# Differential attention scores: the low-part products of two maps moved onto half of the rows each

## The chip, the core and the metric

The kernel runs on one core of a Trainium2 chip. The metric is the device time of one execution in microseconds (us). Five engines work side by side and meet through semaphores: TensorE (PE; its weight loads are shown as PEld), VectorE (DVE), ScalarE (ACT), GpSimd (POOL) and SyncE (SP, which here issues all DMA transfers).

## What is computed

One encoder layer over 1280 tokens (1024 of a prompt, 256 of a sample) of width 1024. The change touches the scores of the differential attention: eight heads, each with two maps `c`, and per map a product of queries and keys over a head width of 64.

```python
def diff_attention(q, k, v, lam):            # q, k: (B, T, 8 heads, 2 maps, 64)
    ...
        s = jnp.einsum('bqhcd,bkhcd->bhcqk', qblk, k).astype(jnp.float32)
        p = jax.nn.softmax(s, axis=-1)
        p = p[:, :, 0] - lam * p[:, :, 1]
        return jnp.einsum('bhqk,bkhe->bqhe', p.astype(v.dtype), v)
```

## The kernel before

Every float32 operand is held as two float32r parts, a high one and a low one with `x = high + low`, and a product is built in PSUM from matmuls of such parts. An earlier stage writes queries and keys to DRAM as `qd[n]` and `kd[n]`, with n = 0 for the high parts and n = 1 for the low ones.

The attention stage goes over 40 pairs: per head four blocks of 256 prompt queries against 1024 keys, and one block of 256 sample queries against 256 keys. Each pair is two units of 128 queries, so there are 64 wide units and 16 narrow ones. `Pair.scores` makes the scores of one unit (both maps), `probs` the softmax, the difference and the transposes, and `values` the product with the values of a pair four units later.

For the scores the head width of 64 fills only half of the 128 rows of the array, so high and low parts are stacked. `load_keys` makes one key tile per map, high keys on rows 0 to 63 and low keys on rows 64 to 127. `load_queries` makes two query tiles, each `[128, 2, 256]` with one plane per map: in `Q[0]` the high queries stand on both halves of the rows, in `Q[1]` the low queries do. One matmul with `Q[0]` (line 741) gives high x high + high x low, and one with `Q[1]` (line 742) gives low x high + low x low. A wide map has two key blocks of 512, so a wide unit has eight score matmuls of 128x512, all over 128 rows.

A map's scores stand in a PSUM tile of two banks; the pool `ps_s` has two such tiles, one per map. DVE takes the row maximum (line 743), then ACT the exponential (line 745), after which the tile is free.

Beside the attention run the fillers: matrix products that the attention doesn't need (lines 283, 286 and 287, in `gemm_fm`), which are dealt out between units by a budget of time per unit (`fill`). The first matmul of each is held behind `anchor[0]`, the last line-741 matmul that was written. The final order on each engine is set by the framework's scheduler, which takes what is ready in its own model of time, so the source order of a unit isn't the order on PE.

Of the kernel before, what the change touches and what calls it, by code (L numbers as in the profile page):

```python
# [9 lines left out]
F32 = mybir.dt.float32  # L10
F32R = mybir.dt.float32r
# [40 lines left out]
QB = 3  # L52
# [88 lines left out]
def encoder_layer_kernel(ctx: ExitStack, tc: tile.TileContext, i, y_out):  # L141
    nc = tc.nc
    V, S, G, PE, SP = nc.vector, nc.scalar, nc.gpsimd, nc.tensor, nc.sync
# [9 lines left out]
    def f32(ap):  # L153
        return ap.bitcast(F32)
# [4 lines left out]
    def dt_(name, shape):  # L159
        return dram.tile(shape, F32, tag=name, name=name)  # L160


    qd = dt_("qd", [2, NB, 128, T])
    kd = dt_("kd", [2, NB, 128, T])
# [27 lines left out]
    def pool(es, name, bufs, space=None, side=None):  # L192
        kw = {} if space is None else {"space": space}
        if side is not None:
            kw["side"] = side
        return es.enter_context(tc.tile_pool(name=name, bufs=bufs, reuse_waits="tile", **kw))
# [194 lines left out]
    def load_keys(h):  # L391
        K = []
        for c in range(2):
            hc = 2 * h + c
            k = kp.tile([128, T], F32R, tag="k", name="k")
            for n in range(2):
                SP.dma_start(f32(k[n * 64:n * 64 + 64]), kd[n, :, hc * 8:hc * 8 + 8, :])
            K.append(k)
        return (K,)

    def load_queries(h, q0):
        qs = []
        for m in range(2):
            z = kp.tile([128, 2, 256], F32R, tag=f"q{m}", name="q", bufs=QB)
            for half in (slice(0, 64), slice(64, 128)):
                for c in range(2):
                    hc = 2 * h + c
                    SP.dma_start(f32(z[half, c, :]), qd[m, :, hc * 8:hc * 8 + 8, q0:q0 + 256])
            qs.append(z)
        return qs  # L410

    def load_values(h):
# [10 lines left out]
    with ExitStack() as es:  # L423
# [188 lines left out]
        for n, (kind, b) in enumerate(steps):  # L612
            if n >= 3:
                if kind in FN:
                    plain(kind, b)
                elif kind == "v":
                    values_out(b)
                else:
                    heads_out(kind, b)
            if n == 4:  # L620
                for c, (h, l, w_) in enumerate(xop):
                    for m, z in enumerate((h, l)):
                        for k in range(0, 8, 4):
                            SP.dma_start(xd[m, k:k + 4, :, cs(c)].rearrange("k p t -> p k t"), f32(z[:, k:k + 4, :]))
            if n == 5:
                for k in range(0, 8, 2):
                    raw, h, l = (rot.tile([128, 2, M], d, tag=t, name="m" + t) for t, d in (("tab", F32), ("o", F32R), ("z", F32R)))
                    SP.dma_start(raw, i["memT"][:, k:k + 2, :])
                    split(h, l, raw, S, V)
                    for m, z in enumerate((h, l)):  # L630
                        SP.dma_start(memd[m, k:k + 2].rearrange("k p t -> p k t"), f32(z))
            if n in LRUAT:
                with tc.high_priority(offset=-LRUP):
                    recur(LRUAT.index(n))
            if n == HEADAT:
                lru.close()
                kp = pool(head_pools, "kq", KB, side="right")
                wv = pool(es, "wv", 3, side="right")
                heads[0] = load_keys(0)
                queries_of[0] = load_queries(0, 0)  # L640
# [18 lines left out]
    with ExitStack() as es:  # L659
# [11 lines left out]
        ps_s = pool(es, "psS", 2, PSUM)  # L671
# [38 lines left out]
        anchor = [None]  # L710
# [10 lines left out]
        class Pair:  # L721
            def __init__(self, h, q0, s0, nk):
                self.h, self.q0, self.s0, self.nk = h, q0, s0, nk
                self.nkt = nk // 128
                self.nth = (self.nkt + 3) // 4
                self.E = {}

            def scores(self, qt):
                K = self.ops[0]
                Q = self.Q  # L730
                nk = self.nk
                qs = slice(qt * 128, qt * 128 + 128)
                nm = sp.tile([128, 2], F32, tag="nm", name="nm")
                ss = sp.tile([128, 2], F32, tag="ss", name="ss")
                E = []
                for c in range(2):
                    ps = ps_s.tile([128, 1024], F32, tag="s", name="s")
                    for k0 in range(0, nk, 512):
                        n = min(512, nk)
                        ks = slice(self.s0 + k0, self.s0 + k0 + n)  # L740
                        anchor[0] = PE.matmul(ps[:, k0:k0 + n], Q[0][:, c, qs], K[c][:, ks], start=True, stop=False)
                        PE.matmul(ps[:, k0:k0 + n], Q[1][:, c, qs], K[c][:, ks], start=False, stop=True)  # L742
                    V.tensor_reduce(nm[:, c:c + 1], ps[:, :nk], axis=AX.X, op=ALU.max, negate=True)  # L743
                    e = ep.tile([128, 1024], F32, tag=f"e{c}", name="e")
                    S.activation(e[:, :nk], ps[:, :nk], AF.Exp, bias=nm[:, c:c + 1], accum_out=ss[:, c:c + 1])  # L745
                    E.append(e)
                self.E[qt] = (E, ss)

            def probs(self, qt):
                nk, nkt, nth = self.nk, self.nkt, self.nth  # L750
                E, ss = self.E.pop(qt)
                if qt == 0:
# [7 lines left out]
                V.scalar_tensor_tensor(self.s1q[:, qt:qt + 1], ss[:, 0:1], 1e-5, ss[:, 0:1], ALU.mult, ALU.mult)  # L760
                V.scalar_tensor_tensor(E[0][:, :nk], E[1][:, :nk], r, E[0][:, :nk], ALU.mult, ALU.add)
                for a in range(nth):
                    n = min(4, nkt)
                    ps = ps_t.tile([128, 4, 128], F32, tag="t", name="t")
                    for t in range(n):
                        kt = a * 4 + t
                        PE.transpose(ps[:, t, :], E[0][:, kt * 128:kt * 128 + 128], ident)
                    dh = self.pts[a][0][:, :, qt * 128:qt * 128 + 128]
# [40 lines left out]
        units = [(p, qt) for p in pairs for qt in range(2)]  # L809
        heads[0] += load_values(0)  # L810
        queries_of[1] = load_queries(0, 256)
        with tc.high_priority(offset=MEMP):
            mem = stored(memd, 0, M)
        done = 0.0
        for u in range(len(units) + VLAG):
            if u < len(units):
                p, qt = units[u]
                ahead = units[min(u + LEAD, len(units) - 1)][0].h
                if ahead not in heads:
                    with tc.high_priority(offset=-LOADP):  # L820
                        heads[ahead] = load_keys(ahead)
                later = units[min(u + LEADQ, len(units) - 1)][0]
                n_ = pairs.index(later)
                if n_ not in queries_of:
                    queries_of[n_] = load_queries(later.h, later.q0)
                p.ops = heads[p.h]
                p.Q = queries_of[pairs.index(p)]
                p.scores(qt)
                done += FILLT / 8.5 * (1 if p.nk == TP else 0.25)
            if 1 <= u <= len(units):  # L830
                p, qt = units[u - 1]
                p.probs(qt)
            if VLAG <= u and units[u - VLAG][1] == 1:
                p = units[u - VLAG][0]
                if len(heads[p.h]) == 1:
                    heads[p.h] += load_values(p.h)
                p.ops = heads[p.h]
                p.values()
            fill(done)
# [102 lines left out]
    with ExitStack() as es:  # L942
# [4 lines left out]
        for c0, n in CHUNKS:  # L947
# [5 lines left out]
            for b in range(8):  # L953
# [3 lines left out]
                ps = pp.tile([128, 512], F32, tag="mm", name="ps")[:, :n]  # L957
                for k in range(8):
                    wh, wl = (z[:, k * 128:k * 128 + 128] for z in ws[b])
                    h, l = (op[m][k // 2][:, k % 2, :] for m in range(2))  # L960
# [5 lines left out]
                m = st.tile([128, 2, 512], F32R, tag="m", name="m")[:, :, :n]  # L966
# [8 lines left out]
    with ExitStack() as es:  # L975
# [24 lines left out]
        with ExitStack() as es1:  # L1000
# [3 lines left out]
            kp = pool(es1, "kX", 2)  # L1004
# [4 lines left out]
            ps_s = pool(es1, "psS", 2, PSUM)  # L1009
# [106 lines left out]
    with ExitStack() as es:  # L1116
# [44 lines left out]
        with ExitStack() as es1:  # L1161
# [49 lines left out]
            for half_ in range(2):  # L1211
# [3 lines left out]
                for fs in groups:  # L1215
                    hs_ = []
                    for f in fs:
                        hs_.append(hidden(f, *((E_M1, E_SL1) if f == NF - 1 else (E_M, E_SL))))
                        if pending:
                            z, t = pending.pop()  # L1220
# [100 lines left out]
```

## Time and profile before

| | us |
|---|---|
| median of 3 runs | 2827.26 (2827.05 to 2828.02) |
| profiled execution, its own time | 2822.44 |
| span of that execution | 2820.5 |
| PE busy | 2739.3 (97%) |
| DVE busy | 1705.5 (60%) |
| ACT busy | 1138.6 (40%) |
| POOL busy | 919.3 (33%) |
| granted TensorE clock, mean | 0.993 |

The attention stage runs from 632.78 us (its first score matmul) to about 1333.6 us of the span. A time on PE is best read from the starts of neighbouring matmuls: the duration shown for one matmul reaches past the start of the next, since matmuls are pipelined and their ends are modelled.

### The profile page before, as it was taken

Reading aid. Unit: us, or ns where it says so; the run is one execution under the profiler, and the core shown is the slowest. Engines: PE = TensorE matmul, PEld = TensorE weight load, DVE = VectorE, ACT = ScalarE, POOL = GpSimd, SP = SyncE. Lnnn points to the kernel's source line nnn. Section 1 sums busy time; section 2 is a strip of 40 time slices with the busy share of each in tenths; the row PEclk is TensorE's granted clock in tenths of the full one; section 3 lists DMA queues with packets and bytes.
Section 4 is the critical chain, followed back from the end, with each engine's and each line's share of the span. In section 5 each row is a group of like instructions: output and inputs, shape, how many; then the busy total and the mean of one; then the engine's idle time right before and its main releaser. Section 6 shows DMA issues by size and latency. Waiting matters only on the chain.

```text
span 2820.5 us, 40319 instructions
## 1 busy us (share of the span) xinstructions
PE 2739.3 (97%) x15240; PEld 2411.8 (86%) x15240; DVE 1705.5 (60%) x2517; ACT 1138.6 (40%) x1921; POOL 919.3 (33%) x576
## 2 busy tenths in 40 slices
PE   9999999999999999999999999998999998999998
PEld 7888888887889888888788889887999997899997
DVE  4545667415667755644345576563677777577776
ACT  3656444415666655455211144321223333233232
POOL 0000000013345543344100100052566559565555
PEclk9999999999999999999999999999999999999999
DMA  9633545565567756844887576658322225622221
GB/s 358 208 109 112 175 152 190 174 206 178 162 202 222 244 169 199 252 141 162 303 273 235 172 276 210 217 186 299 116 79 90 83 82 193 227 84 80 79 80 60
DMA packets 292450, 496.26 MB, mean 176 GB/s; under 512 B 22560, under 2 KB 165664, under 8 KB 292256
## 3 DMA queue, kind: packets, MB, share of 16 engines
q1 hardware_dynamic: 292256, 493.69, 53.6%
q8 instruction: 120, 1.97, 0.3%
q14 instruction: 74, 0.61, 0.1%
HBM read 342.08 MB, written 151.52 MB: 175 GB/s over the span
## 4 chain that ended last, share of the span: by engine, by line
PE 67%; DVE 11%; DMA 11%; issue 4%; ACT 4%; POOL 2%; SPq 1%; DVEq 0%; ACTq 0%; POOLq 0%
PE ps L283 4%; PE ps L286 4%; PE ps L287 4%; PE ps L357 3%; PE ps L355 3%; PE ps L356 3%; PE ps L520 3%; PE ps L521 3%; PE ps L522 3%; PE o L1202 3%; PE o L1203 3%; PE o L1204 2%; PE ps L885 2%; PE ps L883 2%; PE ps L884 2%
## 5 line engine op out<-in xcount | busy, mean ns | idle before, releaser
L190 POOL TENSOR_TENSOR wl<-raw,wh 128x1024 fp32r<-128x1024 f32 x132 | 321.3, 2435 | 973.5 <-ACT wh L187 863.6
L187 ACT ACTIVATE wh<-raw 128x1024 fp32r<-128x1024 f32 (+1 forms) x224 | 224.4, 1006 | 492.0 <-PE ps L286 155.2
L520 PE MATMUL ps<-xh,wh 128*128 128x512 f32 (+1 forms) x768 | 274.4, 357 | 12.1 <-ACT xh L187 5.9
L355 PE MATMUL ps<-xbh,sh 128*128 128x320 f32 x880 | 273.1, 310 | 8.9 <-DMA sh<-fpd 7.0
L521 PE MATMUL ps<-xl,wh 128*128 128x512 f32 (+1 forms) x768 | 273.9, 357 | 0.5 <-DVE xl L190 0.5
L357 PE MATMUL ps<-xbh,sl 128*128 128x320 f32 x880 | 272.6, 310 | 0.4 <-DMA sl<-fpd 0.3
L522 PE MATMUL ps<-xh,wl 128*128 128x512 f32 (+1 forms) x768 | 273.0, 356 | 0.0
L356 PE MATMUL ps<-xbl,sh 128*128 128x320 f32 x880 | 272.4, 310 | 0.0
L283 PE MATMUL ps<-fh,wh 128*128 128x512 f32 (+1 forms) x704 | 258.6, 367 | 11.7 <-DVE g L705 5.0
L286 PE MATMUL ps<-fl,wh 128*128 128x512 f32 (+1 forms) x704 | 255.7, 363 | 2.5 <-DMA fl<-memd 2.5
L287 PE MATMUL ps<-fh,wl 128*128 128x512 f32 (+1 forms) x704 | 255.1, 362 | 0.0
L190 DVE TENSOR_TENSOR wl<-raw,wh 128x1024 fp32r<-128x1024 f32 (+1 forms) x136 | 177.5, 1311 | 96.6 <-ACT wh L187 84.7
L743 DVE TENSOR_REDUCE nm<-s 128x1 f32<-128x1024 f32 (+1 forms) x160 | 167.3, 1059 | 93.8 <-PE s L742 93.4
L1205 DVE SCALAR_TENSOR_TENSOR y<-y,o 128x512 f32<-128x512 f32 x200 | 133.5, 681 | 115.4 <-PE o L1204 108.0
L850 POOL TENSOR_TENSOR rstd<-rstd,mhalf 128x1 f32<-128x1 f32 x30 | 34.5, 1152 | 498.4 <-DVE rstd L849 498.4
L1202 PE MATMUL o<-wh,hh 128*128 128x512 f32 x440 | 175.0, 398 | 11.8 <-DVE wh L189 4.3
L745 ACT ACTIVATE e<-s,nm 128x1024 f32<-128x1024 f32 (+1 forms) x160 | 158.6, 996 | 57.6 <-DVE nm L743 55.7
L355 PEld LDWEIGHTS ps<-xbh,sh 128*128 128x128 f32 x880 | 165.8, 188 | 12.8 <-DMA sh<-fpd 8.4
L520 PEld LDWEIGHTS ps<-xh,wh 128*128 128x128 f32 x768 | 146.3, 190 | 34.3 <-ACT xh L187 5.9
L1203 PE MATMUL o<-wl,hh 128*128 128x512 f32 x440 | 173.1, 394 | 0.0
L356 PEld LDWEIGHTS ps<-xbl,sh 128*128 128x128 f32 x880 | 165.9, 189 | 3.8
L357 PEld LDWEIGHTS ps<-xbh,sl 128*128 128x128 f32 x880 | 165.7, 188 | 3.4 <-DMA sl<-fpd 0.9
(261 smaller groups left out, 7241.6 us busy)
## 6 DMA issues: line engine op xcount, KB each, us to landing
raw<-w_in SPq DMA_DIRECT2D x80, 512.0 KB
raw<-ffn_in SPq DMA_DIRECT2D x80, 512.0 KB
raw<-ffn_out SPq DMA_DIRECT2D x44, 512.0 KB
q<-qd SPq DMA_DIRECT2D x320, 64.0 KB
raw<-p_lru SPq DMA_DIRECT2D x24, 512.0 KB
qd<-hl SPq DMA_DIRECT2D x16, 640.0 KB
kd<-hl SPq DMA_DIRECT2D x16, 640.0 KB
vd<-v SPq DMA_DIRECT2D x40, 256.0 KB
```

The costliest lines, as they stand in the source:

```text
L190: leng.tensor_tensor(l, src, f32(h), ALU.subtract)
L283: ins = PE.matmul(ps, a, h, start=(k == 0), stop=False)
L286: PE.matmul(ps, a, l, start=False, stop=False)
L287: PE.matmul(ps, b, h, start=False, stop=(k == 7))
L355: PE.matmul(ps, w[n][0][:, ks], xb[m][0][:, k, :], start=(k == 0), stop=False)
L356: PE.matmul(ps, w[n][0][:, ks], xb[m][1][:, k, :], start=False, stop=False)
L357: PE.matmul(ps, w[n][1][:, ks], xb[m][0][:, k, :], start=False, stop=(k == 3))
L520: PE.matmul(ps, wh[:, ks], h[:, k, :], start=(k == 0), stop=False)
L521: PE.matmul(ps, wh[:, ks], l[:, k, :], start=False, stop=False)
L522: PE.matmul(ps, wl[:, ks], h[:, k, :], start=False, stop=(k == 7))
L1202: PE.matmul(ps, hs_[a][0][:, ts], wo[a][0][:, hs], start=(a == 0), stop=False)
L1203: PE.matmul(ps, hs_[a][0][:, ts], wo[a][1][:, hs], start=False, stop=False)
```

## The change

The low products are made on 64 rows instead of 128. The low queries of both maps stand in one tile: those of map 0 on rows 0 to 63, those of map 1 on rows 64 to 127. The keys of map 1 are stacked the other way, low keys on top and high keys below, so that each map's high keys lie on the same rows as its low queries. A low product then multiplies low queries with high keys alone; the term low x low is no longer computed. The number of score matmuls stays the same: four of 128 rows and four of 64 rows in a wide unit, two and two in a narrow one. Both PSUM tiles of a unit are taken ahead of its matmuls, the source writes all four high products first, then the low ones alternating between the maps, and after them the two row maxima and exponentials. A pair's queries come in six transfers instead of eight.

```diff
             k = kp.tile([128, T], F32R, tag="k", name="k")
             for n in range(2):
-                SP.dma_start(f32(k[n * 64:n * 64 + 64]), kd[n, :, hc * 8:hc * 8 + 8, :])
+                half = n if c == 0 else 1 - n
+                SP.dma_start(f32(k[half * 64:half * 64 + 64]), kd[n, :, hc * 8:hc * 8 + 8, :])
...
-        for m in range(2):
-            z = kp.tile([128, 2, 256], F32R, tag=f"q{m}", name="q", bufs=QB)
-            for half in (slice(0, 64), slice(64, 128)):
-                for c in range(2):
-                    hc = 2 * h + c
-                    SP.dma_start(f32(z[half, c, :]), qd[m, :, hc * 8:hc * 8 + 8, q0:q0 + 256])
-            qs.append(z)
+        zh = kp.tile([128, 2, 256], F32R, tag="qh", name="q", bufs=QB)
+        zl = kp.tile([128, 256], F32R, tag="ql", name="q", bufs=QB)
+        for n, half in enumerate((slice(0, 64), slice(64, 128))):
+            for c in range(2):
+                hc = 2 * h + c
+                SP.dma_start(f32(zh[half, c, :]), qd[0, :, hc * 8:hc * 8 + 8, q0:q0 + 256])
+            hc = 2 * h + n
+            SP.dma_start(f32(zl[half]), qd[1, :, hc * 8:hc * 8 + 8, q0:q0 + 256])
+        qs = [zh, zl]
...
+                pss = [ps_s.tile([128, 1024], F32, tag="s", name="s") for c in range(2)]
                 for c in range(2):
-                    ps = ps_s.tile([128, 1024], F32, tag="s", name="s")
-                    for k0 in range(0, nk, 512):
-                        n = min(512, nk)
-                        ks = slice(self.s0 + k0, self.s0 + k0 + n)
-                        anchor[0] = PE.matmul(ps[:, k0:k0 + n], Q[0][:, c, qs], K[c][:, ks], start=True, stop=False)
-                        PE.matmul(ps[:, k0:k0 + n], Q[1][:, c, qs], K[c][:, ks], start=False, stop=True)
+                    for k0, ks in keys:
+                        anchor[0] = PE.matmul(pss[c][:, k0:k0 + n], Q[0][:, c, qs], K[c][:, ks], start=True, stop=False)
+
+                for k0, ks in keys:
+                    for c, half in enumerate((slice(0, 64), slice(64, 128))):
+                        PE.matmul(pss[c][:, k0:k0 + n], Q[1][half, qs], K[c][half, ks], start=False, stop=True)
+                for c, ps in enumerate(pss):
                     V.tensor_reduce(nm[:, c:c + 1], ps[:, :nk], axis=AX.X, op=ALU.max, negate=True)
```

In the changed kernel the high products are line 743 and the low products line 747; the transposes of line 767 are line 773, and the value products of lines 785 to 787 are lines 791 to 793.

The order on PE at the second unit of the program, before. In the names `s_` is a map's PSUM tile, `k_4249` and `k_4252` are the keys of map 0 and map 1, and of the two `q_` tiles the first holds high queries and the second low ones:

```order
L286 MATMUL ps_5047<-fl_4969,wh_5042 128x512
L741 MATMUL s_5086<-k_4249,q_4255 128x512
L742 MATMUL s_5086<-k_4249,q_4260 128x512
L741 MATMUL s_5086<-k_4249,q_4255 128x512
L742 MATMUL s_5086<-k_4249,q_4260 128x512
L287 MATMUL ps_5047<-fh_4965,wl_5043 128x512
L741 MATMUL s_5094<-k_4252,q_4255 128x512
L742 MATMUL s_5094<-k_4252,q_4260 128x512
```

The same unit on PE in the changed kernel:

```order
L286 MATMUL ps_5041<-fl_4965,wh_5036 128x512
L743 MATMUL s_5078<-k_4249,q_4255 128x512 x2
L747 MATMUL s_5078<-k_4249,q_4256 128x512 x2
L287 MATMUL ps_5041<-fh_4961,wl_5037 128x512
L743 MATMUL s_5079<-k_4252,q_4255 128x512 x2
L747 MATMUL s_5079<-k_4252,q_4256 128x512 x2
L773 MATMUL t_5104<-ident_80,e_4995 128x128 x4
```

Here the two low products of one map follow each other, and those of the other map come later, behind a filler and that map's high products; the alternation of the source isn't kept.

A later unit on PE, before:

```order
L741 MATMUL s_7246<-k_6189,q_6586 128x512
L742 MATMUL s_7246<-k_6189,q_6591 128x512
L741 MATMUL s_7246<-k_6189,q_6586 128x512
L742 MATMUL s_7246<-k_6189,q_6591 128x512
L741 MATMUL s_7254<-k_6192,q_6586 128x512
L742 MATMUL s_7254<-k_6192,q_6591 128x512
```

The same unit on PE in the changed kernel, with map 0's tile `s_7220` and map 1's `s_7221`:

```order
L743 MATMUL s_7220<-k_6171,q_6566 128x512 x2
L743 MATMUL s_7221<-k_6174,q_6566 128x512 x2
L747 MATMUL s_7220<-k_6171,q_6567 128x512
L747 MATMUL s_7221<-k_6174,q_6567 128x512
L747 MATMUL s_7220<-k_6171,q_6567 128x512
L747 MATMUL s_7221<-k_6174,q_6567 128x512
L773 MATMUL t_7097<-ident_80,e_6895 128x128 x4
```

Here the order of the source is kept: the four low products stand together and alternate between the halves of the rows.

Over the whole stage the 256 wide low products stand on PE in 115 unbroken runs: 81 of two of the same map, 16 of four that alternate, 6 of three that alternate and 12 of one. The 32 narrow low products stand in 27: 22 of one and 5 of two, one of each map. A run is followed and preceded by matmuls over 128 rows; there are 142 in all.

## Rows read from the trace of the kernel before

**Rows 1.** The page: engine totals, then PE and its granted clock in 40 slices.

```profile
PE 2739.3 (97%) x15240; PEld 2411.8 (86%) x15240; DVE 1705.5 (60%) x2517; ACT 1138.6 (40%) x1921; POOL 919.3 (33%) x576
...
PE   9999999999999999999999999998999998999998
...
PEclk9999999999999999999999999999999999999999
```

**Rows 2.** Busy time by stretch: attention stage, then the stretch behind it.

```profile
core 0: us, PE busy (x) PEld busy (x) DVE busy (x) ACT busy (x) POOL busy (x), PEclk, DMA share, GB/s
632.78:1333.60 700.82, 687.95 (x4071) 600.72 (x4070) 417.00 (x680) 414.91 (x789) 304.98 (x179) 1.00 0.62 192
1333.60:1420.00 86.40, 79.49 (x367) 64.62 (x366) 34.50 (x46) 21.36 (x31) 15.16 (x11) 0.98 0.89 312
```

**Rows 3.** What PE waited for, 620 to 1335 us.

```profile
engine line waited for: us in total, times, longest us
PE pm L799 <- POOL rs L797: 2.9, 1, 2.9
PE ps L286 <- DMA fl<-memd: 2.5, 3, 0.9
PE ps L283 <- ACT mst L680: 1.5, 1, 1.5
PE ps L283 <- DMA fh<-xd: 1.3, 1, 1.3
PE ps L283 <- DMA fh<-lrud: 1.1, 3, 0.5
PE o L787 <- DMA vl<-vd: 1.0, 2, 0.8
```

**Rows 4.** Groups of PE instructions by line and shape, 632 to 1336 us.

```profile
L741 PE MATMUL s<-k,q 128*128 128x512 f32 x256 | 106.2, 415 | 1.0 <-DVE v L190 0.5 <-ACT e L745 0.4
L742 PE MATMUL s<-k,q 128*128 128x512 f32 x256 | 100.9, 394 | 0.0
...
L742 PE MATMUL s<-k,q 128*128 128x256 f32 x32 | 8.7, 283 | 0.0
```

**Rows 5.** PE in order of time: start us, duration us, then the instruction.

```profile
800.30 0.40 PE L742 MATMUL s<-k,q 128*128 128x512 f32 x1
800.54 0.28 PE L786 MATMUL o<-ptl,vh 128*128 128x256 f32 x1
...
801.38 0.28 PE L787 MATMUL o<-pth,vl 128*128 128x256 f32 x1
801.50 0.60 PE L686 MATMUL ps<-ident,mst 128*128 128x128 f32 x4
...
805.63 0.39 PE L283 MATMUL ps<-fh,wh 128*128 128x512 f32 x1
...
806.09 0.39 PE L287 MATMUL ps<-fh,wl 128*128 128x512 f32 x1
...
811.07 0.38 PE L799 MATMUL pm<-ident,rs 128*128 128x128 f32 x2
```

**Rows 6.** PE's weight loads in order of time, same columns.

```profile
805.86 0.19 PEld L287 LDWEIGHTS ps<-fh,wl 128*128 128x128 f32 x1
806.09 0.19 PEld L283 LDWEIGHTS ps<-fh,wh 128*128 128x128 f32 x1
```

**Rows 7.** PE in order of time behind a wait.

```profile
814.01 0.50 PE L741 MATMUL s<-k,q 128*128 128x512 f32 x1 [0.40 <-ACT e L745]
814.34 0.40 PE L742 MATMUL s<-k,q 128*128 128x512 f32 x1
```

**Rows 8.** The row maxima and the exponentials, each line's instructions: min/median/max ns.

```profile
L743 DVE TENSOR_REDUCE nm<-s x160: 410/1215/1226, 634.2 to 1331.5; 128x1 f32<-128x1024 f32 x128, 128x1 f32<-128x256 f32 x32
...
L745 ACT ACTIVATE e<-s,nm x160: 474/1117/1187, 647.6 to 1333.0; 128x1024 f32<-128x1024 f32 x128, 128x256 f32<-128x256 f32 x32
```

**Rows 9.** SP's issues of the query loads: min/median/max ns.

```profile
L408 SPq DMA_DIRECT2D q<-qd x320: 574/575/3442, 550.0 to 1276.8; - x160
```

More of the change, by code (lines that the diff above doesn't have):

```diff
@@ L401, in load_queries @@
     def load_queries(h, q0):
-        qs = []
-        for m in range(2):
-            z = kp.tile([128, 2, 256], F32R, tag=f"q{m}", name="q", bufs=QB)
-            for half in (slice(0, 64), slice(64, 128)):
-                for c in range(2):
-                    hc = 2 * h + c
-                    SP.dma_start(f32(z[half, c, :]), qd[m, :, hc * 8:hc * 8 + 8, q0:q0 + 256])
-            qs.append(z)
+        zh = kp.tile([128, 2, 256], F32R, tag="qh", name="q", bufs=QB)
[7 more added lines that the diff above has]
+        qs = [zh, zl]
         return qs
@@ L735, in scores @@
                 E = []
+                n = min(512, nk)
+                keys = [(k0, slice(self.s0 + k0, self.s0 + k0 + n)) for k0 in range(0, nk, 512)]
+                pss = [ps_s.tile([128, 1024], F32, tag="s", name="s") for c in range(2)]
                 for c in range(2):
-                    ps = ps_s.tile([128, 1024], F32, tag="s", name="s")
-                    for k0 in range(0, nk, 512):
-                        n = min(512, nk)
-                        ks = slice(self.s0 + k0, self.s0 + k0 + n)
-                        anchor[0] = PE.matmul(ps[:, k0:k0 + n], Q[0][:, c, qs], K[c][:, ks], start=True, stop=False)
-                        PE.matmul(ps[:, k0:k0 + n], Q[1][:, c, qs], K[c][:, ks], start=False, stop=True)
+                    for k0, ks in keys:
[4 more added lines that the diff above has]
+                for c, ps in enumerate(pss):
                     V.tensor_reduce(nm[:, c:c + 1], ps[:, :nk], axis=AX.X, op=ALU.max, negate=True)
```

## The prediction

> **What bounds the kernel now.** I read the engine totals first, then the stage, then PE's waits, then single matmuls. PE is busy in every slice of the span and its clock is at the higher level, 2.4 GHz, throughout [rows 1]. In the attention stage PE is busy for 687.95 of 700.82 us, while no other compute engine reaches 420 us [rows 2]. So the stage is a queue of PE work with 12.9 us of gaps in it. The table of waits says what the gaps are: singles of one to three microseconds, on a transfer, on POOL or on ACT, and none on the scores [rows 3]. A nanosecond that PE saves or loses in this stage therefore moves the end by about as much, and whatever happens on the other engines has to be large to count.
>
> What one matmul costs is read from starts, not from durations. Between 805.63 and 811.07 stand 24 matmuls of 512 columns, so one takes 5.44 / 24 = 0.227 us [rows 5]. Eight of 256 columns stand between 800.54 and 801.50, so one takes 0.12 us [rows 5]. The duration shown is 0.394 us [rows 4], so each matmul reaches 0.394 - 0.227 = 0.167 us into its successor; I call this its tail. The weight load of 0.19 us starts with the matmul ahead of its own and lies under it: the load for line 283 starts at 806.09, together with the line-287 matmul ahead of it [rows 5, 6]. Where no matmul covers it, it shows: behind a wait, a matmul of 512 columns at 814.01 is followed by the next at 814.34, which is 0.33 us instead of 0.227, so an uncovered load costs 0.10 us [rows 7].
>
> **The change part by part.** The number of score matmuls, their columns and their loads stay the same: 256 wide and 32 narrow low products before and after [rows 4]. Halving the rows of a matmul does not shorten it, as far as columns set the time: the 512 and the 256 columns above differ as their columns do. A gain can come only where two low products on different halves of the rows run at the same time.
>
> *How many can.* The source alternates the maps, but the order on PE decides, and there most low products of one map stand by themselves. From the runs counted in the section on the change, 16 of four give two such pairs each and 6 of three give one each: 38 wide pairs out of 128 possible. The 5 narrow pairs gain nothing that counts, because two loads take as long as two narrow matmuls: 0.12 us each is already what a matmul with its load takes. If a pair runs in the time of one matmul, the gain is 38 x 0.227 = 8.6 us. If it does not, the gain is 0.
>
> *What a switch costs.* There are 142 runs of low products, each entered from and left to matmuls over all 128 rows. That makes 284 places at which the array goes from one form to the other; the kernel before has none, its score rows all read 128*128 [rows 4]. This is the unknown price. The bound from below is 0: when the kind of operand changes, from a value product at 801.38 to a transpose at 801.50, the distance is the ordinary 0.12 us, so PE can change kind without a pause [rows 5]. The bound from above is a complete stop: the new form enters only when the tail of the old one is out, 0.167 us, and only then does its load begin, another 0.10 us, together 0.267 us. In between lie the two single prices: a load that can't be laid under a matmul of the other form, 0.10 us, or a tail that must run out while the load lies under it, 0.167 us. A change of form is unlike a change of operand kind: sums that ran through 128 rows have to leave after 64, while the matmul ahead is still in the same rows. That is why I do not take 0. The nearest rows are the two single prices, and I take their middle, 0.13 us: 284 x 0.13 = 36.9 us. The ends are 0 and 284 x 0.267 = 75.8 us.
>
> The Trainium skill, page "TensorEngine Tiling (Array Packing)", section Key Properties, says that changing the tiling mode, not just the tile, drains TensorE; it speaks against this change, gives no duration, and no run so far shows such a drain. The same page's table of speedups allows up to two times for a contraction of 64 rows; by it all 128 pairs would give 128 x 0.227 = 29.1 us, and this order on PE has only 38 of them.
>
> *PSUM tiles and the row maxima.* In the 16 alternating wide units map 0's row maximum starts some four matmuls later, about 0.9 us, than it did. Who waits: DVE's maximum (1.215 us), then ACT's exponential (1.117 us), then the next unit's first high product into that tile [rows 8]. PE has values, transposes and fillers to do in between, and no wait on the scores is among its longer ones [rows 3]. DVE and ACT are idle for 280 us each in the stage [rows 2]. Cost 0; if the cover failed in all 16 units it would be 16 x 0.9 = 14 us, which I hold unlikely.
>
> *Query loads.* Six transfers per pair instead of eight, 80 fewer; at 0.575 us each this takes 46 us off SP's queue [rows 9]. The weights of the fillers and the values stand in that queue, so they start earlier. PE's waits on transfers are fl 2.5, fh 1.3 and 1.1 and vl 1.0, together 5.9 us [rows 3]; that is the most it can give. These are first loads of a stage and not late queries, so I take 0. The keys stacked the other way are as many transfers of the same size.
>
> *Order.* The scheduler moves fillers by some places. The 12.9 us of gaps may come out a few microseconds smaller or larger, and a later stage end can lay up to some 5 of the 6.9 us that PE is idle in the stretch behind it under other work [rows 2]. I take 0, and about 4 us either way.
>
> **The sum.** 36.9 - 8.6 = +28.3 us, all in the attention stage. The profiled execution would go from 2822.4 to 2850.7 us. Its own time lies 4.8 us below the median of the runs, so the median goes from 2827.3 to about 2855 us. The single prices give the forecast's own range: 284 x 0.10 - 8.6 = +19.8 and 284 x 0.167 - 8.6 = +38.8, that is 2847 to 2866 us.
>
> **The rivals.**
>
> *A switch costs nothing and pairs run together (faster).* The mechanism is in the 38 pairs: 8.6 us less, 2818.7 us. For it speaks that PE changes between transposes, value products and scores without a pause [rows 5]. Against it speaks that none of those changes the rows in use. It decides below 8.6 / 284 = 0.030 us per switch; above that the change loses.
>
> *A switch is a complete stop.* 284 x 0.267 - 8.6 = +67.2 us, 2894 us. For it: after a wait PE does show the load uncovered [rows 7], and if a load of the other form may not enter rows in use, it comes behind the tail. Against it: loads are otherwise started a whole matmul ahead [rows 6].
>
> *The change does not do what it says.* PE goes on issuing one matmul after the other, without a stop and without running two at once: 0, 2827 us. For it: each low product has its own load, and two loads take 0.24 us, as long as one wide matmul, so the pair could be held up by its loads. Without pairs but with a switch price the time would be 2864 us, inside the forecast's own range.
>
> **How the numbers follow.** The forecast, a switch price somewhere around the two single prices, has a chance of 0.45; the complete stop 0.20; no price with pairs 0.20; nothing at all 0.15. About 0.2% of the time, 5.7 us, is what a measurement of this kernel can tell from no change. Slower: the forecast and the complete stop and a sliver of the rest, 0.66. Faster: most of the free pairs, 0.17. Same: nothing at all, and prices near the break-even, 0.17. The predicted time is the forecast's, 2855 us. To leave out no more than 2 in 10 the range has to reach from the free pairs to the complete stop, 2817 to 2895 us.
>
> **What would show it.** In the profile after, the step from a high product (line 743) to a low one (line 747), and from a low one to the next matmul over 128 rows, should be some 0.33 to 0.39 us instead of 0.227. Two low products of the same map should stand 0.227 us apart. In an alternating run the second product should start almost with the first, and the third about 0.23 us after it. The attention stage should end near 1362 us instead of 1333.6, with DVE, ACT and POOL busy as long as before. Steps of 0.227 everywhere would refute the switch price; 0.49 would be the complete stop. Wrong in another way would be low products that take longer than 0.227 us each, or new waits of PE on ACT at line 743: then the PSUM tiles, not the rows, would be what costs.

## The result and the profile after

The changed kernel takes 2857.66 us (median of 4 runs, 2856.66 to 2859.75), the kernel before beside it 2827.58 us: a ratio of 1.0111 (95% interval 1.0099 to 1.0123), 30 us more. The prediction was 2855 us, slower.

The engine totals of the changed kernel; against [rows 1] PE is 46 us busier, and no other engine by more than about 1 us:

```profile
PE 2785.0 (97%) x15240; PEld 2395.8 (84%) x15240; DVE 1703.2 (60%) x2517; ACT 1139.7 (40%) x1921; POOL 914.7 (32%) x576
```

The attention stage, from the first score matmul on, and the stretch behind it, with the columns of [rows 2]:

```profile
core 0: us, PE busy (x) PEld busy (x) DVE busy (x) ACT busy (x) POOL busy (x), PEclk, DMA share, GB/s
629.95:1374.00 744.05, 734.90 (x4079) 583.40 (x4078) 417.54 (x681) 417.05 (x789) 303.29 (x180) 1.00 0.57 177
1374.00:1460.00 86.00, 84.09 (x398) 69.65 (x399) 34.11 (x49) 21.82 (x33) 13.94 (x9) 1.00 0.87 309
```

About as many PE instructions as before (4079 against 4071) now need 744 us instead of 701, at the same clock, and DVE, ACT and POOL are busy as long as before [rows 2]. The time is lost on PE, in this stage.

Where it is lost stands in the order of time. First a run of two low products of the same map, PE and then its weight loads (start us, duration us; "x2" is two instructions in one row):

```profile
656.85 0.39 PE L287 MATMUL ps<-fh,wl 128*128 128x512 f32 x1
657.07 0.61 PE L743 MATMUL s<-k,q 128*128 128x512 f32 x2
657.62 0.73 PE L747 MATMUL s<-k,q 64*128 64x512 f32 x2
658.27 0.50 PE L283 MATMUL ps<-fh,wh 128*128 128x512 f32 x1
658.61 0.40 PE L286 MATMUL ps<-fl,wh 128*128 128x512 f32 x1
```

```profile
656.85 0.41 PEld L743 LDWEIGHTS s<-k,q 128*128 128x128 f32 x2
657.62 0.29 PEld L747 LDWEIGHTS s<-k,q 64*128 64x128 f32 x2 [0.35 <-issue]
658.27 0.19 PEld L283 LDWEIGHTS ps<-fh,wh 128*128 128x128 f32 x1 [0.36 <-issue]
658.38 0.19 PEld L286 LDWEIGHTS ps<-fl,wh 128*128 128x128 f32 x1
```

Two high products take 657.62 - 657.07 = 0.55 us instead of 2 x 0.227, and the two low ones 658.27 - 657.62 = 0.65 instead of 0.45; the filler behind them takes 0.34 instead of 0.227. The load rows say why. In [rows 6] a load starts a whole matmul ahead of its own. Here the load of the first low product starts only at 657.62, together with its matmul, after PEld stood still for 0.35 us; the load of the first matmul over 128 rows does the same at 658.27. So at a change of form no load starts under the matmul ahead: PE goes some 0.09 us past the ordinary step, and then loads without cover. In this trace the load starts together with its own matmul at all 284 switches. From the starts of single matmuls (the rows merge them), this run reads 0.319, 0.335, 0.322 and 0.337 us, where 0.227 each would be ordinary: 0.092 + 0.108 us for going in and 0.095 + 0.110 us for coming out, 0.20 us per switch. Over all 142 runs the median price of a run, with the gain of its pairs added back, is 0.41 us.

A run of four that alternate between the halves, PE and then its weight loads:

```profile
806.61 0.73 PE L747 MATMUL s<-k,q 64*128 64x512 f32 x4
807.28 0.66 PE L773 MATMUL t<-ident,e 128*128 128x128 f32 x4
```

```profile
806.61 0.30 PEld L747 LDWEIGHTS s<-k,q 64*128 64x128 f32 x4 [0.36 <-issue]
```

Four products take 0.67 us, as long as the two above: the second of each pair starts 3 or 4 ns after the first, and their four loads are through in 0.30 us, like the two above in 0.29. Pairs do run at the same time.

**Bookkeeping for all kernels below.** On PE I add up the distances from start to start in the attention stage, up to the first matmul of the merge stage behind it, and take off an ordinary distance for each matmul (0.227, 0.118, 0.109 and 0.11 us for 512, 256, 128 and 1 columns). What is left at the steps into, within and out of runs of low products over 64 rows, the step behind the first matmul after a run among them, I call their net cost, gains from pairs included; what is left anywhere else I call gaps. Before: gaps 35.3 us. After: net cost 48.0 us, gaps 21.4 us. These gaps are not the 12.9 us of the prediction: those are PE's idle time up to 1333.6 us, while the stage here reaches to 1393.9 us and every step over the ordinary one counts. PE's idle time alone is 19.8 us before and 11.1 us after in this longer stage.

### The profile page after: what moved, and what is told of

It is laid out like the page before. It is cut to its first block, busy times and chain, and to the rows that moved or that the text cites. A ratio compares the mean times of both kernels' runs of the same rounds, so it can differ in the third digit from the quotient of the medians.

```text
span 2858.0 us, 40191 instructions
## 1 busy us (share of the span) xinstructions
PE 2785.0 (97%) x15240; PEld 2395.8 (84%) x15240; DVE 1703.2 (60%) x2517; ACT 1139.7 (40%) x1921; POOL 914.7 (32%) x576
## 4 chain that ended last, share of the span: by engine, by line
PE 73%; DVE 10%; DMA 7%; issue 4%; ACT 3%; POOL 3%; SPq 0%; DVEq 0%; POOLq 0%; ACTq 0%
PE ps L283 5%; PE ps L286 5%; PE ps L287 5%; PE ps L523 3%; PE ps L522 3%; PE ps L524 3%; PE ps L355 3%; PE ps L357 3%; PE ps L356 3%; PE s L747 3%; PE o L1208 3%; PE o L1209 2%; PE o L1210 2%; PE ps L889 2%; PE ps L890 2%
```

## The experiments

Unless said otherwise, times are medians beside the kernel before on the same chip, with 95% intervals of the ratio.

### The order alone, over all rows (e1_all_rows)

```diff
 # changed kernel, with load_keys and load_queries of before
                 for k0, ks in keys:
-                    for c, half in enumerate((slice(0, 64), slice(64, 128))):
-                        PE.matmul(pss[c][:, k0:k0 + n], Q[1][half, qs], K[c][half, ks], start=False, stop=True)
+                    for c in range(2):
+                        PE.matmul(pss[c][:, k0:k0 + n], Q[1][:, c, qs], K[c][:, ks], start=False, stop=True)
```

> The changed kernel's way of writing a unit (both PSUM tiles taken first, four high products, then the low ones alternating, then the maxima), but with the loads of before and every low product over all 128 rows: no switch of form, no pairs. Theory 1, the price is in the rows (0.20 us per switch, 284 switches, pairs together): 2827.6 us, no change. Theory 2, part of the time is in the order (PE's gaps in the stage fell by 14 us in the trace of the changed kernel): about 2814 us. Theory 3, the loss comes from taking both PSUM tiles at once and the later row maxima, not from the rows: about 2858 us.

Measured: 2833.27 us against 2830.32, 1.0011 (1.0001 to 1.0022). Theory 3 falls: taking both PSUM tiles first and the maxima later costs 3 us, not 30. Theory 2 falls too: the gaps in the stage are 42.0 us, not shorter than before but longer. Part of that is the clock. In four stretches of this stage, 17.1 us together, the granted clock is 0.50, the lower level of 1.2 GHz, and wide matmuls stand 0.427 us apart instead of 0.227; before there is one such stretch, of 3.4 us. Half of PE's busy time in these stretches is an estimate of what that costs: 6.6 us of the gaps here and 1.7 us before. The loss is in the rows.

### Three ways of placing the low products (e2_pairs, e3_per_map, e4_each)

In each of these three every score matmul is tied to the one ahead of it by an order dependency; only the sequence differs.

```diff
+                def behind(ins, prev):
+                    if prev is not None:
+                        tc.add_manual_dep(ins.ins, prev.ins.name, ORDER, reason="order")
+                    return ins
 # e2_pairs:   A high, A high, B high, B high, A low, B low, A low, B low
 # e3_per_map: A high, A high, A low, A low, then the same of B
 # e4_each:    A high, A low, A high, A low, then the same of B
```

> The changed kernel with its score matmuls tied to the order of the source, so that nearly all low products of different halves stand side by side: 89 runs, 122 wide and 16 narrow pairs on PE, instead of 142 runs with 38 and 5. Theory 1: 89 x 0.405 - 122 x 0.227 - 16 x 0.11 = +6.5 us, 2834 us. With theory 2's shorter gaps on top: 2820 us. Theory 3 (PSUM tiles held longer, and here always): slower than the changed kernel, over 2858 us.

> The changed kernel with the low products of each map tied directly behind its own high ones: 162 runs of low products and no pairs on different halves. Theory 1: 162 x 0.405 = +65.6 us, 2893 us. With theory 2's shorter gaps: 2879 us. Theory 3 (each map's maximum starts as early as before): back to about 2828 us.

> The changed kernel with every low product tied directly behind its own high one, the order of before on PE: 288 runs of one low product, 576 switches, no pairs. Theory 1: 288 x 0.405 = +116.6 us, 2944 us. With theory 2's gaps, if they belong to the order of the changed kernel, no difference from that. Theory 3: about 2828 us.

Measured, against 2830.32 us: e2_pairs 2842.10 us, 1.0046 (1.0028 to 1.0065); e3_per_map 2879.89 us, 1.0182 (1.0166 to 1.0198); e4_each 2926.29 us, 1.0345 (1.0327 to 1.0363). The time rises with the number of runs and falls with the number of pairs, and theory 3's "back to 2828" is out by 52 and 98 us. Theory 1's price holds on PE: net cost 7.0 us for 89 runs with 29.6 us gained by pairs, 66.8 us for 162 runs, 119.6 us for 288 runs; with the gains added back 0.411, 0.412 and 0.415 us per run, for the changed kernel (48.0 + 9.2) / 142 = 0.403. At the end, though, 12, 50 and 96 us arrive, not 7, 67 and 120. Most of the difference is in the gaps: 43.3, 22.6 and 19.9 us, against 35.3 before.

In e4_each both kinds of score matmul carry the price, since each stands next to a switch (PE groups of that kernel: busy us, mean ns; the means of before are 394 and 415 in [rows 4]):

```profile
L750 PE MATMUL s<-k,q 64*128 64x512 f32 x256 | 127.0, 496 | 0.0
L749 PE MATMUL s<-k,q 128*128 128x512 f32 x256 | 122.4, 478 | 0.0
```

### Neighbours on the same half (e5_same_half)

```diff
 # as e2_pairs, with load_keys and load_queries of before
-                        ... Q[1][half, qs], K[c][half, ks] ...
+                        ... Q[1][0:64, c, qs], K[c][0:64, ks] ...
```

> As e2_pairs (score matmuls tied to the order of the source, low products of both maps alternating), but the low products of both maps lie on rows 0 to 63, with the key tiles and query loads of before: 91 runs, and neighbours that share their rows. If halves on different rows run together and halves on the same rows do not: 91 x 0.405 = +36.9 us, some 8 to 14 us of it covered by shorter gaps, 2853 to 2865 us, against +12 us of e2_pairs. If it is the short rows alone that made e2_pairs cheap: as e2_pairs, about 2842 us.

Measured: 2873.78 us against 2826.52, 1.0172 (1.0157 to 1.0188), 47 us, and some 35 more than e2_pairs. What makes a pair cheap is the other half of the array, not the shorter product. A run of four here, on PE:

```profile
681.46 1.20 PE L751 MATMUL s<-k,q 64*128 64x512 f32 x4
682.59 0.66 PE L777 MATMUL t<-ident,e 128*128 128x128 f32 x4
```

Four products on the same rows take 1.13 us where four on alternating halves took 0.67: two matmuls more, 0.46 us. The net cost is 36.9 us, as expected; the cover that I expected on top was not there, with gaps of 42.2 us.

### Only where it could pay (e6_wide_only)

Low products tied together in the wide units, four in a run, and left over 128 rows in the narrow ones.

```diff
+            for c in (range(2) if q0 == TP else (n,)):      # load_queries: both maps on both halves
...
+                        if nk < 512:
+                            PE.matmul(pss[c][:, k0:k0 + n], Q[1][:, c, qs], K[c][:, ks], start=False, stop=True)
...
+                with tc.high_priority(offset=400):
+                  for k0, ks in (keys if nk > 512 else ()):
+                    for c, half in enumerate((slice(0, 64), slice(64, 128))):
+                        prev = behind(PE.matmul(pss[c][:, k0:k0 + n], Q[1][half, c, qs], K[c][half, ks], start=False, stop=True), prev)
```

> The changed kernel with its low products tied together in all 64 wide units (64 runs of four, 128 pairs) and the narrow units' low products over all 128 rows: 64 x 0.41 - 128 x 0.227 = -2.9 us of work on PE. Price of the switches alone: about 2827 us, no change that can be told. If tying both PSUM tiles' products together makes PE wait for exponentials, as six waits on ACT of 3.4 us in e2_pairs suggest: 2835 to 2845 us.

Measured: 2834.66 us against 2826.52, 1.0031 (1.0021 to 1.0041). All 128 wide pairs stand together in 64 runs and their net cost is -1.5 us: the gain of the pairs just pays the switches. The kernel is still 8 us slower, since its gaps are 45.3 us. The longest of them in PE's table of waits is the one on PSUM tiles that have to be free before the tied products can start:

```profile
PE s L750 <- ACT e L761: 5.0, 10, 1.7
```

That wait is 0.4 us before [rows 4]. So even the best arrangement of this idea that was tried doesn't beat the kernel before.

### Where the gaps went (e7b_more_work to e11_per_map_rows)

The changed kernel pays 48 us and is 30 us slower. Five runs ask what makes its gaps short. First, more work on PE without any switch (e7b_more_work):

```diff
 # kernel before
+                        if nk > 512 and (c, k0) != (1, 512):
+                            PE.matmul(ps[:, k0:k0 + n], Q[0][:, c, qs], K[c][:, ks], start=True, stop=True)
                         anchor[0] = PE.matmul(ps[:, k0:k0 + n], Q[0][:, c, qs], K[c][:, ks], start=True, stop=False)
```

> The kernel before with three of the four high products of a wide unit issued twice, the first one a complete product of its own that the second overwrites: 192 more matmuls of 512 columns over 128 rows, 192 x 0.227 = 43.6 us more work on PE in the attention stage, with no switch of form. Theory 4, gaps give way: when PE has more to do in the stage, transfers and other engines are in time and its gaps shrink from some 35 to some 20 us, so that only about 30 us arrive at the end, about 2860 us. Theory 5, every nanosecond on PE arrives: 2871 to 2874 us, and the shorter gaps of the changed kernel belong to something else.

Measured: 2868.80 us against 2828.51, 1.0139 (1.0122 to 1.0156), 40 of the 43.6 us; gaps 34.0 us. Work that is merely longer arrives at the end nearly whole: theory 4 as I put it falls.

Second, whether the two query transfers less per pair do it (e8_old_loads):

```diff
 # as e3_per_map, with load_keys and load_queries of before
-                        ... Q[1][half, qs], K[c][half, ks] ...
+                        ... Q[1][0:64, c, qs], K[c][0:64, ks] ...
```

> As e3_per_map (low products of each map tied behind its high ones, 64 rows, no pairs), but both maps on rows 0 to 63 with the key tiles and the eight query transfers of before: 163 runs, 163 x 0.41 = +66.8 us of work on PE. Theory 4 (longer work covers gaps, whatever is loaded): as e3_per_map, about +51 us, 2878 us. Theory 6 (the shorter gaps of the changed kernel and of e3_per_map come from two query transfers less per pair): gaps stay near 40 us, 2894 us.

Measured: 2879.34 us against 2828.51, 1.0180 (1.0165 to 1.0195), the same as e3_per_map with six transfers (2879.89); net cost 66.4 us for 163 runs, gaps 23.9 us. With gaps as short as those of e3_per_map, the loads have no part in it.

Third, whether short gaps are chance of an execution: both kernels, unchanged, profiled once more (e9_before_again, e10_after_again).

> The kernel before, unchanged, profiled a second time, to see how far PE's gaps in the attention stage differ between executions of one program. In its first profile they are 35.3 us, and the work behind the stage took 1416 us, 1 to 7 us less than in the other kernels' profiles. If gaps belong to the program: 33 to 38 us again. If they are chance of the execution: anything between 20 and 45 us.

> The changed kernel, unchanged, profiled a second time. In its first profile PE's gaps in the attention stage, steps of low products left out, are 21.4 us. If gaps belong to the program (its order, and switches that cover waits): 19 to 24 us again, and some 30 us over the kernel before. If they are chance of the execution: up to 40 us.

Measured: gaps of 38.9 us before, just over the range expected, and 22.4 us after, net cost 48.1 us, spans of 2824.6 and 2857.2 us. To within 4 us the gaps belong to the program.

Last, a twin of e8_old_loads that differs from it in the rows alone (e11_per_map_rows). The scheduler gives both the same order, row for row, on all five engines (but for two neighbouring rows of DVE at 116 us, long before the stage), so each step on PE can be set against the same step of the other.

```diff
 # as e8_old_loads
-                        ... Q[1][0:64, c, qs], K[c][0:64, ks] ...
+                        ... Q[1][:, c, qs], K[c][:, ks] ...
```

> The very program order of e8_old_loads on every engine (each map's two low products tied behind its two high ones, loads of before), but the low products over all 128 rows: no switch of form. It parts what e8 left open, whose steps around low products cost 66.4 us while its gaps were only 23.9 us. If the short gaps belong to the order: gaps near 24 us again, 12 to 15 us faster than before, about 2814 us. If the stops at the switches cover waits that PE would otherwise have: gaps of 35 to 42 us, about 2829 to 2833 us.

Measured: 2829.03 us against 2828.14, 1.0006 (0.9994 to 1.0018), with gaps of 38.7 us. In the same order, without switches, the long gaps are back. Set step against step, the stage is 816.2 us with switches and 764.5 without, 51.7 us apart, while the steps around low products cost 66.4 us. Of the 14.7 us between, 6.9 stand at those very steps in the twin too, as small delays and short waits that the stop now contains, and 7.8 are gaps elsewhere that got shorter, 31.7 to 23.9 us. By an estimate of the same kind as above 1.7 of the 14.7 us are the clock, which is at the lower level for 10.2 us of the twin's stage and for 6.8 us of the other. PE's waits in the twin, and then in the kernel with switches:

```profile
PE ps L283 <- DVE g L705: 6.0, 6, 2.8
PE pm L807 <- POOL rs L805: 3.0, 1, 3.0
PE ps L283 <- DMA fh<-lrud: 2.7, 4, 1.5
...
PE o L793 <- DMA vh<-vd: 1.5, 1, 1.5
```

```profile
PE ps L283 <- DVE g L705: 6.0, 6, 2.8
...
PE pm L807 <- POOL rs L805: 1.3, 1, 1.3
PE ps L283 <- DMA fh<-lrud: 0.6, 1, 0.6
```

The reading is that POOL and the transfers go on while PE stops for a switch, and that PE finds them further when it gets there, so a switch that stands ahead of a wait is in part paid by that wait. The largest wait of both fits: the 6.0 us on DVE's `g` stand behind the last low product of the stage, and they are not shorter.

## The prediction, step by step

**Its frame held.** The stage is a queue of PE work: PE's own steps account for the loss, the other engines' busy times don't move, and the order of writing by itself is worth 3 us (first experiment) or nothing (twin). One reading of the waits was loose: two short ones, 0.5 and 0.4 us, do stand on the scores [rows 4]; they change nothing.

**The count of pairs held.** 38 wide pairs were counted from the order, and 38 of them start within a few ns of each other. Their gain, 8.6 us, was sized rightly; the 5 narrow pairs, held at nothing, bring another 0.6 us: their two products start 3 to 4 ns apart too, so their loads do not hold them up.

**The price of a switch was too small.** This is the term that was mis-sized: "their middle, 0.13 us: 284 x 0.13 = 36.9 us". Measured it is 0.20 us, 57.2 us in all. The step that failed is the choice between the single prices: both are paid, one after the other, as the rival of the complete stop had it. That rival's sum was too large in turn, 0.267 us, because it took the whole tail of a matmul, 0.167 us, from the durations shown; the stop ahead of the load is only 0.092 to 0.095 us in the run shown, and the load behind it 0.108 to 0.110. What the trace showed of an uncovered load, 0.10 us [rows 7], was right; the modelled end of a matmul was a poor measure of when the next form may enter.

The signs that the prediction named came in part. The steps into and out of a run are some 0.32 us, just under its 0.33 to 0.39. But two low products of the same map stand 0.335 us apart, not 0.227, and the third product of an alternating run 0.34 us behind the first, not 0.23, because the uncovered load shows one step later. The last score matmul starts at 1372.0 us instead of 1331.2, 40.8 us later and not 28.3.

The Trainium skill, page "TensorEngine Tiling (Array Packing)", section Key Properties, says that a change of the tiling mode drains TensorE, and gives no duration. This trace agrees, in that no load of the new form starts under a matmul of the old one; 0.20 us per switch is this kernel's.

**What was held at zero gave the rest back.** Query loads: 0, right (2879.3 and 2879.9 us with eight and six transfers). Row maxima and PSUM tiles in the changed kernel: 0, right; PE's waits on ACT at the scores are 0.5 us there. It becomes 1.9 to 5.0 us where the low products of both maps are tied together (e2_pairs, e5_same_half, e6_wide_only). Order and gaps: "I take 0, and about 4 us either way" was wrong by 10 us: the gaps fell by 13.9 us in one pair of profiles and 16.5 in the other.

The fall has two parts. Some 7.5 of the 13.9 us stand behind the last score matmul, where no switch follows: gaps of 10.6 us before and 3.1 after. The first experiment has no switch at all and 3.3 us there, so this part comes with the order of writing. The prediction had named something like it, as "up to some 5 of the 6.9 us" of idle time behind, and had set it at 0; PE's idle time behind the last score matmul is 6.9 us before, 1.9 after and 2.1 in the first experiment. The wait on `g`, over the whole stage, is a part of it: 5.0 us before, 1.9 after, 2.4 in the first experiment.

The other 6.4 us, 24.7 to 18.3, lie ahead of the last score matmul, among the switches. The chance that part of a stop falls where PE would have waited anyway wasn't in the sum at all.

**So the total was right by two errors that cancel.** In the two profiles: +48.0 us of net cost, -13.9 us of gaps, -2.8 us because the first score matmul starts earlier (629.95 against 632.78), +6.3 us behind the stage; 37.5 us between the spans. Between the second profiles it is 32.6 us, between the medians 30.1. The forecast had +36.9 - 8.6 = +28.3. A sum with the price as measured would have been +48, and with gaps 14 us shorter about +34. That the forecast came within 2 us of the medians' difference is luck: its price was about 20 us too low, and what made up for it was held at zero.

**What is left open.** For the changed kernel itself there is no twin of the same order over all rows: the first experiment comes near it, but its gaps, 42.0 us, hold other waits, such as 6.3 us on `fh<-xd`, and more time at the lower clock. That its gaps ahead of the last score matmul are short for the same reason as those of the twin's partner is argued, not shown. One run speaks against a simple rule: e5_same_half pays 36.9 us of stops, and its gaps, 42.2 us, are as long as those of the first experiment, which has none (its order is another one). Why the stretch before the first score matmul is 2.8 us shorter and that behind the stage 6.3 us longer isn't explained either. Nor is it settled why 43.6 us of plain extra work covered almost nothing; that kernel's order on PE is another one, with new waits on ACT and DVE of 3.8 and 2.5 us.

## What to carry to other kernels

Two products that use different halves of the rows run together if they stand next to each other on PE, but what decides is how often PE changes form: here a run of half-row products costs 0.41 us to enter and leave, so it needs two pairs of 512 columns (0.454 us) just to pay for itself. Read the order on the engine, not the order of the source: the scheduler left 38 of 128 wide pairs standing, and tying all 128 together brought the loss from 30 us to 8 but not to a gain, since the pairs just paid the switches and waits for PSUM tiles came on top. And where an engine's stops stand ahead of waits, part of their price can be paid already (up to 14.7 of 66.4 us against the twin, while e5_same_half, with 36.9 us of stops, has gaps no shorter than before): sum the stops, and then look which waits behind them shrink.

## What the runs showed of the hardware

- A pair on different halves starts mostly 3 to 4 ns apart (1 to 8 ns over the 43 pairs) and takes no longer than one product: four alternating products 0.67 us, four on the same rows 1.13 us. The Trainium skill, page "TensorE: Matmul & The Clock Gate", Part 3, gives about 4 ns between the starts of tiles on different rows; this trace agrees.
- The loads of different halves overlap as the products do: four for alternating halves are through in 0.30 us, two for the same rows in 0.29.
- A change of form keeps PE from loading ahead although nothing is being waited for: 0.20 us per switch, about the same on the way in and on the way out, and in seven kernels between 0.40 and 0.43 us per run. Where transposes follow, the way out costs about 0.15 us.
- It is not the only place where a load isn't covered: behind a row of transposes of 128 columns the second wide matmul stands 0.32 us behind the first in the kernel before too (662.65 and 662.97 us), without a switch or a wait.
